# Encoder trunk, down projection: activation sums of the seven-product pairs made during the up projection and kept in device memory, and eleven such pairs per column group in place of seven

## The chip, the cores and the metric

One core of one Trainium2 chip runs the whole kernel as a single program. The metric is device microseconds from start to end of an execution: before the change 1316.85 to 1317.11 us in three runs, median 1317.1 us. The profiler saw one more execution, with a span of 1314.9 us from the first to the last instruction. PE is the engine that multiplies matrices, DVE and ACT are the two engines that work element by element, POOL is a third one that is here used mainly to issue transfers, and SP issues the loads of the weights. The program lists the instructions of each engine in a fixed order; semaphores make one engine wait for another.

## The reference

One layer of an encoder on 256 positions (T) of 2048 features (D), in float32. What matters here is the last part, the channel mixer:

```python
def conv_ffn(x, g_norm, w_up, conv_k, conv_b, w_down):
    h = rms_norm(x, g_norm)
    up = h @ w_up                                   # 2048 -> 2 * 5504
    pad = jnp.pad(up, ((0, 0), (1, 1), (0, 0)))
    up = (pad[:, :t] * conv_k[0] + pad[:, 1:t + 1] * conv_k[1]
          + pad[:, 2:t + 2] * conv_k[2] + conv_b)
    gate, val = jnp.split(up, 2, axis=-1)
    return x + (jax.nn.silu(gate) * val) @ w_down   # 5504 -> 2048
```

After it comes a last RMSNorm. Ahead of it stands the mixer block (gated MLP, neighbourhood attention, merge, output projection), which the change leaves as it is but for signs in the formulas.

## The kernel before, in words

**Products in float32.** Every operand is split into a high part (rounded to the type that PE takes) and a low part (the rest). ACT writes the high part as a copy (line 151 for weights, tile `whi`), DVE subtracts it from the original for the low part (line 152, tile `wlo`). A product is then three matmuls: high by high, low by high, high by low. In the down projection `triple` (lines 291 to 293) issues the three.

**Units.** The weights come through one list of units. A unit of the down projection is 128 rows of `w_down` by 1024 columns, 512 KB, one load on SP's queue (line 126) into a `wraw` tile. There are five `wraw` tiles and four each of `whi` and `wlo`, used in turn. When the program reaches unit i, `begin(i)` issues first the loads up to unit i+4, then the splits up to unit i+3, and then the extra tasks that were registered for i with `at(i, ...)`. PE's matmuls of unit i follow. So DVE and ACT meet their work in exactly this order, and a split of unit i+3 or i+4 can start only when PE has left the tile of four units earlier.

**The down projection** (`g_dn`, two groups of 1024 columns, 43 units each) accumulates all 43 units in four banks C, one for each half t of the positions and half c of the columns. A plain unit is four triples, 12 matmuls. Two neighbouring units (a *pair*; q is its number in the group, i = n0 + 2q its first unit) form a product of a 2 by 2 by a 2 by 2 block matrix. For the pairs in `DOWN_QUADS` it is made with seven block products in place of eight. Their four sums of activation blocks (`act_sums`, lines 298 to 303, and their split, lines 309 and 310) and four sums of weight blocks (`weight_sums`, lines 316 to 319, and their split, lines 326 and 327, into tiles "13" and "24") are made by DVE and ACT. `run_wide` issues three triples at unit i of such a pair and four at unit i+1, of which the first two use the weight sums "13" and the other two "24". Four more banks, P, accumulate over all the seven-product pairs of the group. After the last such pair `ev_sums` adds P into the residual tile `x2` (lines 909 to 919). At the end of the first group `ev_down` adds C into `x2` (`add_down`, line 1014), and the second group's first matmuls need those banks.

In the file before, the activation sums of a pair are registered for unit i-5, their split for i-4, the weight sums for i-3, and both their splits for i-2. All these tiles lie in single rooms `h0` to `h7`, so a room is written again only after its last reader. The raw weights of a pair stay in `wraw` until the weight sums have read them.

**The up projection** (`g_up`, 22 groups of two 128-column blocks of gate and value, the last one of one) has 8 units a group and, for each group, `ev_up` as tasks in the units after it: the convolution (lines 987 to 994), the gate (lines 999 and 1000), and the split into the activations `a` (lines 485 and 486) that the down projection multiplies.

Of the kernel before, what the change touches and what calls it, by code (L numbers as in the profile page):

```python
# [8 lines left out]
F32 = mybir.dt.float32  # L9
F32R = mybir.dt.float32r  # L10
# [45 lines left out]
OUT_ORDER = (tuple(range(16)), (0, 1, 6, 7, 2, 3, 10, 11, 4, 5, 8, 9, 12, 13, 14, 15))  # L56
TURN_X2 = (13, 1)
Y_GAP = 224
DOWN_QUADS = ((4, 6, 9, 11, 14, 16, 18), (3, 5, 8, 10, 13, 15, 17))


@with_exitstack
def trunk_kernel(ctx, tc, x, norm_mix, w_in, ln_g, ln_b, w_s, b_s, rpb, w_branch, w_out,
# [105 lines left out]
    def at(i, f):  # L169
        tasks.setdefault(i, []).append(f)  # L170
# [93 lines left out]

    def wide(src, row0, order, c0, acts, quads, room, done, sums=None, odd=None):
        n0 = plan_wide(src, row0, order, c0)
        boxes = {}
        for n, q in enumerate(quads):  # L270
            i = n0 + 2 * q
            own = odd if odd and n % 2 else room
            whole[i] = whole[i + 1] = None
            units[i], units[i + 1] = 1, 2
            b = boxes[q] = {}
            if sums is None:
                b["acts"] = {}
                sum_acts_at(i - 5, i - 4, b["acts"], lambda k=order[2 * q]: ff["ap"][k // 2], room, "s")
            else:
                b["acts"] = sums[order[2 * q]]  # L280
            at(i - 3, lambda i=i, b=b: weight_sums(i, b, room))
            at(i - 2, lambda b=b, own=own: weight_sums_split(b, own))
        return ("wide", n0, order, acts, quads, boxes, done)

    def sum_acts_at(i, j, box, pair, room, name):
# [3 lines left out]
    def triple(p, x, h, l, st, sp):  # L289
# [2 lines left out]
        nc.tensor.matmul(p, xl, h, start=False, stop=False)  # L292
        nc.tensor.matmul(p, xh, l, start=False, stop=sp)  # L293

    def act_sums(a, box, room):
        w = room("f", F32)
        f = w[:, 0].rearrange("p (k t) -> p k t", k=2)
        nc.vector.tensor_add(f, a[:, :, 0, :].bitcast(F32), a[:, :, 1, :].bitcast(F32))
        s1, s2, s3, s4 = (w[:, 1, n * 128:(n + 1) * 128] for n in range(4))
        nc.vector.tensor_add(s1, f[:, 0, 128:], f[:, 1, 128:])  # L300
        nc.vector.tensor_sub(s3, f[:, 0, :128], f[:, 0, 128:])
        nc.vector.tensor_sub(s2, s1, f[:, 0, :128])
        nc.vector.tensor_sub(s4, f[:, 1, :128], s2)
        box["w"] = w

    def act_sums_split(box, room, name):
        w = box.pop("w")
        o = room(name, F32R)
        nc.scalar.activation(o[:, 0], w[:, 1], AF.Copy)
        nc.vector.tensor_sub(o[:, 1], w[:, 1], o[:, 0].bitcast(F32))  # L310
        box["s"] = [(o[:, 0, n * 128:(n + 1) * 128], o[:, 1, n * 128:(n + 1) * 128]) for n in range(4)]

    def weight_sums(i, box, room):
        r0, r1 = whole.pop(i), whole.pop(i + 1)
        t13, t24 = room("t13", F32), room("t24", F32)
        nc.vector.tensor_sub(t13[:, 0], r0[:, 1], r0[:, 0])
        nc.vector.tensor_sub(t24[:, 0], r1[:, 1], t13[:, 0])
        nc.vector.tensor_sub(t13[:, 1], r1[:, 1], r0[:, 1])
        nc.vector.tensor_sub(t24[:, 1], r1[:, 0], t24[:, 0])
        box["w"] = (t13, t24)  # L320

    def weight_sums_split(box, room):
        u = []
        for name, t in zip(("13", "24"), box.pop("w")):
            h, l = room("h" + name, F32R), room("l" + name, F32R)
            nc.scalar.activation(h, t, AF.Copy)
            nc.vector.tensor_sub(l, t, h.bitcast(F32))
            u.append((h, l))
        box["t"] = {1: [x[:, 0] for x in u[0]], 3: [x[:, 1] for x in u[0]],
                    2: [x[:, 0] for x in u[1]], 4: [x[:, 1] for x in u[1]]}  # L330

    def run_wide(g, tail=0):
        kind, n0, order, acts, quads, boxes, done = g
        n1 = n0 + len(order)
        P = C = None

        def x_of(k, t):
            a = acts(k)
            return a[:, 0, t * 128:(t + 1) * 128], a[:, 1, t * 128:(t + 1) * 128]

        def plain(i, t, c):
            h, l = split_t[i]
            triple(C[t][c], x_of(order[i - n0], t), h[:, c], l[:, c], i == n0, i == n1 - 1)

        for i in range(n0, n1 - tail):
            begin(i)
            q, r = divmod(i - n0, 2)
            if C is None:
                c = [bank() for _ in range(4)]
                C = [c[:2], c[2:]]  # L350
            if q not in quads:
                for t, c in ((0, 0), (0, 1), (1, 0), (1, 1)) if i > 1 else ((0, 0), (1, 0), (0, 1), (1, 1)):
                    plain(i, t, c)
                split_t.pop(i)
                continue
            st, sp = q == quads[0], q == quads[-1]
            k, k1 = order[2 * q:2 * q + 2]
            if r == 0:
                if st:
                    P = [bank() for _ in range(4)]  # L360
                (h0, l0), (h1, l1) = split_t[i], split_t[i + 1]
                triple(P[0], x_of(k, 0), h0[:, 0], l0[:, 0], st, sp)
                triple(C[0][0], x_of(k1, 0), h1[:, 0], l1[:, 0], False, False)
                triple(C[0][1], boxes[q]["acts"]["s"][3], h1[:, 1], l1[:, 1], False, False)
                split_t.pop(i)
                split_t.pop(i + 1)
                continue
            S, W = boxes[q]["acts"]["s"], boxes[q]["t"]
            triple(P[1], S[0], *W[1], st, sp)
            triple(P[3], S[2], *W[3], st, sp)  # L370
            triple(P[2], S[1], *W[2], st, sp)
            triple(C[1][0], x_of(k1, 1), *W[4], False, False)
            if sp:
                done[0](P, i)
        if not tail:
            done[1](C, n1)
            return
        for t in range(NT):
            for c in range(2):
                for i in range(n1 - tail, n1):  # L380
                    if t == 0 and c == 0:
                        begin(i)
                    plain(i, t, c)
                done[1](C, t, c)
# [140 lines left out]
    def post_sums(P, x, spare):  # L525
        p1, p5, p6, p7 = P
        (x11, x12), (x21, x22) = x
        nc.scalar.activation(x11, p1, AF.Copy)
        nc.vector.tensor_add(spare, p6, x11)
        nc.vector.tensor_add(x12, p5, spare)  # L530
        nc.vector.tensor_add(x21, p7, spare)
        nc.vector.tensor_add(x22, p5, x21)

    def add_sums(ps, x):
        for t in range(NT):
            for c in range(2):
                nc.vector.tensor_add(x[t][c], ps[t][c], x[t][c])

    def ev_v_sums(P, i):
        def go():  # L540
# [358 lines left out]
    def ev_sums(j, room):  # L899
        def done(P, i):  # L900
# [5 lines left out]
            def first_half():  # L906
                ab, cd = room("t13", F32), room("t24", F32)
                m["v"], m["u3"], m["w"] = cd[:, 0], cd[:, 1], ab[:, 0]
                nc.scalar.activation(ab[:, 0], p1, AF.Copy)
                nc.vector.tensor_add(x11, p1, x11)  # L910
                nc.vector.tensor_add(ab[:, 1], p6, ab[:, 0])
                nc.vector.tensor_add(m["v"], p5, ab[:, 1])
                nc.vector.tensor_add(m["u3"], p7, ab[:, 1])
                nc.vector.tensor_add(m["w"], p5, m["u3"])

            def second_half():
                nc.vector.tensor_add(x12, x12, m["v"])
                nc.vector.tensor_add(x21, x21, m["u3"])
                nc.vector.tensor_add(x22, x22, m["w"])

            at(i + 1, first_half)
            at(i + 2, second_half)
# [50 lines left out]
    def ev_up(f0, nb):  # L973
        def done(ps, i):
            n = nb
            a = []
            for p in ps:
                t = tmp.tile([128, T], F32, name="tb", bufs=3)
                nc.scalar.activation(t, p[:, T:], AF.Copy)  # L979
# [18 lines left out]
            def gate(b, g, v):  # L998
                nc.scalar.activation(g, g, AF.Silu)
                nc.vector.tensor_mul(g, g, v)  # L1000
                at(cur[0] + 1, lambda: split_plain(g, ff["a"][f0 + b]))

            at(i + 1, lambda: conv(0))
            if n > 1:
# [128 lines left out]
    for f in range(0, NF, 2):  # L1133
        nb = min(2, NF - f)
        g_up.append(stationary(w_u, 0, KD, f * 128, nb * 128, 2, DFF, lambda k: rs["h", k], ev_up(f, nb)))
    h_room = {n: f"h{i}" for i, n in enumerate(("t13", "t24", "h13", "h24", "l13", "l24", "f", "s"))}

    def down_room(name, dt):
        return hpool.tile([128, 2, 512], dt, name=h_room[name])

    g_dn = [wide(w_d, 0, range(NF), g * 1024, lambda k: ff["a"][k], DOWN_QUADS[g], down_room,
                 (ev_sums(2 * g, down_room), ev_down if g == 0 else finish)) for g in range(2)]


    preload[0] = [lambda: load_x(0, 256)]
    for n, (c, _) in enumerate(X_TURN[1:]):
# [102 lines left out]
    ctx.push(fa_st)  # L1249
    ff["ap"] = [fa.tile([128, min(2, NF - k), 2, T], F32R, name=f"a{k // 2}") for k in range(0, NF, 2)]  # L1250
    ff["a"] = [ff["ap"][k // 2][:, k % 2] for k in range(NF)]
    fc = {}

    def open_conv():
# [54 lines left out]
```

## Time and profile before

| | |
|---|---|
| time, median of 3 runs | 1317.1 us (1316.85 to 1317.11) |
| profiled execution, first to last instruction | 1314.9 us |
| PE busy | 1303.3 us, 6776 matmuls |
| DVE busy | 1066.2 us |
| ACT busy | 764.8 us |
| POOL busy | 88.3 us |
| down projection on PE, start of the first and of the last matmul | 1080.30 us and 1305.36 us of the span |
| loads of `w_down` | 86 of 512 KB, median 4.6 us from issue to landing |
| granted PE clock | 0.998 of full speed over the span |

The busy time of an engine is the time in which one of its instructions ran. Matmuls overlap, so PE's busy time hides gaps shorter than a matmul's own length. A row of a timeline has the start in us from the beginning of the span, the length in us, the engine, the line of the file, the operation, the tiles out<-in, the shapes and the number of instructions; in brackets the idle time of the engine before it and whom it waited for. A row of the groups has the count, the busy time and the mean length in ns.

### The profile page before, as it was taken

How to read it: one execution, taken by the hardware profiler on the slowest of the kernel's cores; microseconds unless marked ns; L12 is line 12 of the kernel's file. 1: busy time of each engine (PE TensorE's matmuls, PEld its weight loads, DVE VectorE, ACT ScalarE, POOL GpSimd, SP SyncE). 2: the span in 40 equal slices, each digit the busy share in tenths (PEclk: the TensorE clock that was granted, in tenths of full speed). 3: DMA queues.
4: the chain of work that ended last, by engine and by line, in shares of the span. 5: the costliest groups of instructions: out<-in, count | busy, mean ns of one | idle time of the engine just before them, and what ended most of it. 6: DMA issues, size and time to landing. Idle time of an engine off the chain costs nothing.

```text
span 1314.9 us, 19329 instructions
## 1 busy us (share of the span) xinstructions
PE 1303.3 (99%) x6776; PEld 1112.0 (85%) x6776; DVE 1066.2 (81%) x1625; ACT 764.8 (58%) x1139; POOL 88.3 (7%) x176
## 2 busy tenths in 40 slices
PE   9999999999999999999999999999999999999997
PEld 7888888888888888888888888888888888888885
DVE  7996778667789966986777778787878789999997
ACT  5766476666645644556555555555656556555653
POOL 0004505323000000000000000000000000000000
PEclk9999999999999999999999999999999999999999
DMA  8768656556556657665565665656565656666663
GB/s 305 260 209 235 201 174 201 181 163 194 179 172 209 210 190 241 204 210 163 175 202 182 192 193 182 195 184 193 180 205 177 198 154 226 220 194 206 210 202 119
DMA packets 170577, 259.37 MB, mean 197 GB/s; under 512 B 12664, under 2 KB 124144, under 8 KB 170480
## 3 DMA queue, kind: packets, MB, share of 16 engines
q1 hardware_dynamic: 166448, 250.31, 59.4%
q0 software_dynamic: 3712, 7.30, 2.4%
q8 instruction: 53, 0.87, 0.3%
q10 hardware_dynamic: 320, 0.53, 0.1%
q14 instruction: 44, 0.36, 0.1%
HBM read 253.90 MB, written 2.10 MB: 195 GB/s over the span
## 4 chain that ended last, share of the span: by engine, by line
PE 97%; DVE 1%; ACT 0%; issue 0%; DMA 0%; ACTq 0%; DVEq 0%
PE bank L205 31%; PE bank L209 16%; PE bank L293 12%; PE bank L291 12%; PE bank L292 12%; PE bank L233 5%; PE bank L235 4%; PE bank L234 4%; PE bank L761 1%; DVE wlo L152 0%; PE bank L811 0%; PE bank L503 0%; PE bank L627 0%; PE bank L801 0%; PE bank L892 0%
## 5 line engine op out<-in xcount | busy, mean ns | idle before, releaser
L152 DVE TENSOR_TENSOR wlo<-wraw,whi 128x1024 fp32r<-128x1024 f32 (+1 forms) x472 | 550.3, 1178 | 188.7 <-ACT whi L151 92.0
L151 ACT ACTIVATE whi<-wraw 128x1024 fp32r<-128x1024 f32 (+1 forms) x472 | 472.0, 1015 | 204.7 <-PE bank L292 75.2
L205 PE MATMUL bank<-h,whi 128*128 128x512 f32 x1760 | 426.0, 392 | 0.0
L205 PEld LDWEIGHTS bank<-h,whi 128*128 128x128 f32 x1760 | 321.9, 188 | 62.0 <-DVE ya L631 0.3
L209 PEld LDWEIGHTS bank<-h,wlo 128*128 128x128 f32 x1760 | 225.9, 191 | 8.8
L209 PE MATMUL bank<-h,wlo 128*128 128x256 f32 x1760 | 228.6, 283 | 0.0
L989 ACT ACTIVATE tc<-ta,ck 128x256 f32<-128x256 f32 x86 | 47.1, 594 | 117.1 <-DVE ta L987 117.1
L293 PE MATMUL bank<-wlo,a 128*128 128x512 f32 x260 | 101.5, 390 | 0.2 <-DVE wlo L152 0.2
L292 PE MATMUL bank<-whi,a 128*128 128x512 f32 x260 | 101.2, 389 | 0.0
L291 PE MATMUL bank<-whi,a 128*128 128x512 f32 x260 | 101.2, 389 | 0.0
L291 PE MATMUL bank<-whi,h 128*128 128x512 f32 x204 | 80.3, 393 | 0.0
L292 PE MATMUL bank<-whi,h 128*128 128x512 f32 x204 | 79.5, 390 | 0.0
L293 PE MATMUL bank<-wlo,h 128*128 128x512 f32 x204 | 79.5, 390 | 0.0
L293 PEld LDWEIGHTS bank<-wlo,a 128*128 128x128 f32 x260 | 48.8, 188 | 11.2 <-DVE wlo L152 1.3
L292 PEld LDWEIGHTS bank<-whi,a 128*128 128x128 f32 x260 | 48.8, 188 | 10.3
L291 PEld LDWEIGHTS bank<-whi,a 128*128 128x128 f32 x260 | 48.8, 188 | 10.1
L992 DVE SCALAR_TENSOR_TENSOR tc<-ta,ck,tc 128x255 f32<-128x255 f32 x86 | 41.4, 481 | 14.5 <-ACT tc L989 14.5
L979 ACT ACTIVATE tb<-bank 128x256 f32<-128x256 f32 x86 | 28.3, 385 | 42.2 <-PE bank L205 42.2
L233 PE MATMUL bank<-whi,y 128*128 128x512 f32 x128 | 50.5, 394 | 0.0
L233 PE MATMUL bank<-whi,h 128*128 128x512 f32 x128 | 50.4, 394 | 0.0
L235 PE MATMUL bank<-wlo,h 128*128 128x512 f32 x128 | 49.9, 390 | 0.0
L235 PE MATMUL bank<-wlo,y 128*128 128x512 f32 x128 | 49.9, 390 | 0.0
(299 smaller groups left out, 1744.1 us busy)
## 6 DMA issues: line engine op xcount, KB each, us to landing
wraw<-in_w_up_dram SPq DMA_DIRECT2D x336, 256.0 KB, 3.2
wraw<-in_w_in_dram SPq DMA_DIRECT2D x111, 512.0 KB, 4.5
wraw<-in_w_down_dram SPq DMA_DIRECT2D x86, 512.0 KB, 4.6
wraw<-in_w_in_dram SPq DMA_DIRECT2D x66, 256.0 KB, 3.2
wraw<-in_w_branch_dram SPq DMA_DIRECT2D x32, 512.0 KB, 4.5
wraw<-in_w_out_dram SPq DMA_DIRECT2D x32, 512.0 KB, 3.6
xs<-in_x_dram SPq DMA_DIRECT2D x8, 256.0 KB, 7.6
vw<-y POOLq DMA_DIRECT2D x16, 128.0 KB, 6.9
```

Of the source, the lines that this page charges most:

```text
L151: nc.scalar.activation(h[:, k, :m], w[:, k, :m], AF.Copy)
L152: nc.vector.tensor_sub(l[:, k, :m], w[:, k, :m], h[:, k, :m].bitcast(F32))
L205: nc.tensor.matmul(p, h[:, k - k0, b * 128:(b + 1) * 128], acts(k), start=k == 0, stop=k == nk - 1)
L209: nc.tensor.matmul(p[:, :T], l[:, k - k0, b * 128:(b + 1) * 128], acts(k)[:, 0, :], start=False, stop=False)
L233: nc.tensor.matmul(p, xh, h[:, kk, :m], start=st, stop=False)
L234: nc.tensor.matmul(p, xl, h[:, kk, :m], start=False, stop=False)
L235: nc.tensor.matmul(p, xh, l[:, kk, :m], start=False, stop=sp)
L291: nc.tensor.matmul(p, xh, h, start=st, stop=False)
L292: nc.tensor.matmul(p, xl, h, start=False, stop=False)
L293: nc.tensor.matmul(p, xh, l, start=False, stop=sp)
L989: nc.scalar.activation(v, u, AF.Identity, scale=ck[:, 1, ch:ch + 1], bias=ck[:, 3, ch:ch + 1])
L992: nc.vector.scalar_tensor_tensor(v[:, 1:], u[:, :T - 1], ck[:, 0, ch:ch + 1], v[:, 1:], op0=OP.mult, op1=OP.add)
```

## The change

- The four activation sums of eleven pairs (3, 5, 7, 8, 10, 12, 13, 15, 16, 18, 19 of the 21, `DOWN_PAIRS`) are made once, in the up projection, from the gated activation before its split: four 128-column operations (`act_blocks`), a split into a 128 x 2 x 512 tile (`split_plain`), and a transfer of 512 KB on POOL's queue to a tensor in device memory. These are tasks two and three units after the gate of the pair's second block.
- In both groups of the down projection these pairs take seven products. Before unit i-4 of each, `stored` loads the 512 KB of sums on POOL's queue, into room `h6` or `h7` in turn. The activation sums and their split are gone from the down projection.
- Before, there were seven seven-product pairs per group; now eleven. Some of them follow directly on one another: 7 and 8, 12 and 13, 15 and 16, 18 and 19 in the first group, 7 and 8, 12 and 13, 17 and 18 (by position) in the second. For the second of two such neighbours (`late`) the weight sums are tasks of unit i-1 in place of i-3, and the splits of "13" and "24" are tasks of units i-1 and i in place of i-2.
- The second group takes the pairs of rows in another order (`down_order`), so that its seven-product positions meet the kept pairs.
- The formulas have other signs: additions of weight blocks where there were subtractions, and signs taken back when P is added. The number of operations and their shapes are the same.
[...]

The diff, cut to its core:

```diff
-DOWN_QUADS = ((4, 6, 9, 11, 14, 16, 18), (3, 5, 8, 10, 13, 15, 17))
+DOWN_PAIRS = (3, 5, 7, 8, 10, 12, 13, 15, 16, 18, 19)
+DOWN_QUADS = (DOWN_PAIRS, (1, 3, 5, 7, 8, 10, 12, 13, 15, 17, 18))
...
-            if sums is None:
+            late = q - 1 in quads
             b = boxes[q] = {}
+            if stored:
                 b["acts"] = {}
-                sum_acts_at(i - 5, i - 4, b["acts"], lambda k=order[2 * q]: ff["ap"][k // 2], room, "s")
+                at(i - 4, lambda b=b, k=order[2 * q]: stored(k // 2, b["acts"]))
...
-            at(i - 3, lambda i=i, b=b: weight_sums(i, b, room))
-            at(i - 2, lambda b=b, own=own: weight_sums_split(b, own))
+            at(i - 1 if late else i - 3, lambda i=i, b=b: weight_sums(i, b, room))
+            for h in range(2):
+                at(i - 1 + h if late else i - 2, lambda b=b, own=own, h=h: weight_sums_split(b, own, h))
...
+    def act_blocks(w, a11, a21, a12, a22):
+        s3, n1, p2, s4 = (w[:, n * 128:(n + 1) * 128] for n in range(4))
+        nc.vector.tensor_sub(s3, a11, a21)
+        nc.vector.tensor_sub(n1, a22, a21)
+        nc.vector.tensor_add(p2, n1, a11)
+        nc.vector.tensor_sub(s4, a12, p2)
...
-        nc.vector.tensor_sub(t13[:, 0], r0[:, 1], r0[:, 0])
-        nc.vector.tensor_sub(t24[:, 0], r1[:, 1], t13[:, 0])
-        nc.vector.tensor_sub(t13[:, 1], r1[:, 1], r0[:, 1])
-        nc.vector.tensor_sub(t24[:, 1], r1[:, 0], t24[:, 0])
+        nc.vector.tensor_add(t13[:, 0], r0[:, 0], r0[:, 1])
+        nc.vector.tensor_add(t24[:, 1], t13[:, 0], r1[:, 1])
+        nc.vector.tensor_add(t13[:, 1], r0[:, 1], r1[:, 1])
+        nc.vector.tensor_add(t24[:, 0], r1[:, 0], t24[:, 1])
...
+    def weight_sums_split(box, room, n):
+        t, name = box["w"][n], ("13", "24")[n]
+        h, l = room("h" + name, F32R), room("l" + name, F32R)
+        nc.scalar.activation(h, t, AF.Copy)
+        nc.vector.tensor_sub(l, t, h.bitcast(F32))
...
+                if b and f0 // 2 in ff["kept"]:
+                    at(cur[0] + 2, sums)
+                    at(cur[0] + 3, sums_split)
...
+            def sums():
+                own["w"] = ff["more"].tile([128, 512], F32, name="sw")
+                act_blocks(own["w"], *(own[k][:, t * 128:(t + 1) * 128] for k in range(2) for t in range(2)))
+
+            def sums_split():
+                o = ff["more"].tile([128, 2, 512], F32R, name="so")
+                split_plain(own["w"], o)
+                nc.gpsimd.dma_start(ff["kept"][f0 // 2], o.bitcast(F32))
...
+    def stored(pair, box):
+        n = ff["turn"] = ff.get("turn", -1) + 1
+        o = down_room(f"s{n % 2}", F32R)
+        nc.gpsimd.dma_start(o.bitcast(F32), ff["kept"][pair])
+        box["s"] = sums_of(o)
...
+    dram = keep("dram", space=bass.MemoryType.DRAM)
+    ff["kept"] = {p: dram.tile([128, 2, 512], F32, name=f"sums{p}") for p in DOWN_PAIRS}
...
-    nc = _bacc.Bacc("TRN2", target_bir_lowering=False, num_devices=1)
+    nc = _bacc.Bacc("TRN2", target_bir_lowering=False, num_devices=1, dynamic_dma_scratch_size=4096)
```

More of the change, by code (lines that the diff above doesn't have):

```diff
@@ L262, in run_group, with wide @@
             done(ps, b)
-    def wide(src, row0, order, c0, acts, quads, room, done, sums=None, odd=None):
+    def wide(src, row0, order, c0, acts, quads, room, done, sums=None, odd=None, stored=None):
         n0 = plan_wide(src, row0, order, c0)
@@ L298, in act_sums @@
         nc.vector.tensor_add(f, a[:, :, 0, :].bitcast(F32), a[:, :, 1, :].bitcast(F32))
[L299 to L303, printed above, removed]
+        act_blocks(w[:, 1], *(f[:, k, t * 128:(t + 1) * 128] for k in range(2) for t in range(2)))
         box["w"] = w
@@ L310, in act_sums_split, with sums_of @@
         nc.vector.tensor_sub(o[:, 1], w[:, 1], o[:, 0].bitcast(F32))
-        box["s"] = [(o[:, 0, n * 128:(n + 1) * 128], o[:, 1, n * 128:(n + 1) * 128]) for n in range(4)]
+        box["s"] = sums_of(o)
+    def sums_of(o):
+        return [(o[:, 0, n * 128:(n + 1) * 128], o[:, 1, n * 128:(n + 1) * 128]) for n in range(4)]
     def weight_sums(i, box, room):
@@ L315, in weight_sums @@
         t13, t24 = room("t13", F32), room("t24", F32)
[L316 to L319, printed above, removed]
+        nc.vector.tensor_add(t13[:, 0], r0[:, 0], r0[:, 1])
+        nc.vector.tensor_add(t24[:, 1], t13[:, 0], r1[:, 1])
+        nc.vector.tensor_add(t13[:, 1], r0[:, 1], r1[:, 1])
+        nc.vector.tensor_add(t24[:, 0], r1[:, 0], t24[:, 1])
         box["w"] = (t13, t24)
[L322 to L330, printed above, removed]
+    def weight_sums_split(box, room, n):
[3 more added lines that the diff above has]
+        nc.vector.tensor_sub(l, t, h.bitcast(F32))
+        box.setdefault("t", {}).update({m: (h[:, c], l[:, c]) for c, m in enumerate(((1, 3), (4, 2))[n])})
     def run_wide(g, tail=0):
@@ L368, in run_wide @@
             S, W = boxes[q]["acts"]["s"], boxes[q]["t"]
-            triple(P[1], S[0], *W[1], st, sp)
-            triple(P[3], S[2], *W[3], st, sp)
-            triple(P[2], S[1], *W[2], st, sp)
+            triple(P[1], S[1], *W[1], st, sp)
+            triple(P[3], S[0], *W[3], st, sp)
+            triple(P[2], S[2], *W[2], st, sp)
             triple(C[1][0], x_of(k1, 1), *W[4], False, False)
@@ L528, in post_sums @@
         nc.scalar.activation(x11, p1, AF.Copy)
-        nc.vector.tensor_add(spare, p6, x11)
+        nc.vector.tensor_sub(spare, x11, p6)
         nc.vector.tensor_add(x12, p5, spare)
@@ L536, in add_sums @@
             for c in range(2):
-                nc.vector.tensor_add(x[t][c], ps[t][c], x[t][c])
+                (nc.vector.tensor_sub if c else nc.vector.tensor_add)(x[t][c], ps[t][c], x[t][c])
     def ev_v_sums(P, i):
@@ L910, in first_half @@
                 nc.vector.tensor_add(x11, p1, x11)
-                nc.vector.tensor_add(ab[:, 1], p6, ab[:, 0])
+                nc.vector.tensor_sub(ab[:, 1], ab[:, 0], p6)
                 nc.vector.tensor_add(m["v"], p5, ab[:, 1])
@@ L916, in second_half @@
             def second_half():
-                nc.vector.tensor_add(x12, x12, m["v"])
+                nc.vector.tensor_sub(x12, x12, m["v"])
                 nc.vector.tensor_add(x21, x21, m["u3"])
-                nc.vector.tensor_add(x22, x22, m["w"])
+                nc.vector.tensor_sub(x22, x22, m["w"])
             at(i + 1, first_half)
@@ L976, in done @@
             a = []
+            own = {}
             for p in ps:
@@ L1001, in gate @@
                 at(cur[0] + 1, lambda: split_plain(g, ff["a"][f0 + b]))
+                own[b] = g
+                if b and f0 // 2 in ff["kept"]:
[8 more added lines that the diff above has]
+                nc.gpsimd.dma_start(ff["kept"][f0 // 2], o.bitcast(F32))
             at(i + 1, lambda: conv(0))
@@ L1135, in trunk_kernel, with down_order @@
         g_up.append(stationary(w_u, 0, KD, f * 128, nb * 128, 2, DFF, lambda k: rs["h", k], ev_up(f, nb)))
-    h_room = {n: f"h{i}" for i, n in enumerate(("t13", "t24", "h13", "h24", "l13", "l24", "f", "s"))}
+    h_room = {n: f"h{i}" for i, n in enumerate(("t13", "t24", "h13", "h24", "l13", "l24", "s0", "s1"))}
     def down_room(name, dt):
         return hpool.tile([128, 2, 512], dt, name=h_room[name])
-    g_dn = [wide(w_d, 0, range(NF), g * 1024, lambda k: ff["a"][k], DOWN_QUADS[g], down_room,
-                 (ev_sums(2 * g, down_room), ev_down if g == 0 else finish)) for g in range(2)]
+    def stored(pair, box):
+        n = ff["turn"] = ff.get("turn", -1) + 1
+        o = down_room(f"s{n % 2}", F32R)
+        nc.gpsimd.dma_start(o.bitcast(F32), ff["kept"][pair])
+        box["s"] = sums_of(o)
+    def down_order(g):
+        free = [p for p in range(NF // 2) if p not in DOWN_PAIRS]
+        kept = list(DOWN_PAIRS)
+        pairs = [(kept if q in DOWN_QUADS[g] else free).pop(0) for q in range(NF // 2)]
+        return tuple(2 * p + kk for p in pairs for kk in range(2)) + (NF - 1,)
+    g_dn = [wide(w_d, 0, down_order(g), g * 1024, lambda k: ff["a"][k], DOWN_QUADS[g], down_room,
+                 (ev_sums(2 * g, down_room), ev_down if g == 0 else finish), stored=stored) for g in range(2)]
+    dram = keep("dram", space=bass.MemoryType.DRAM)
+    ff["kept"] = {p: dram.tile([128, 2, 512], F32, name=f"sums{p}") for p in DOWN_PAIRS}
     preload[0] = [lambda: load_x(0, 256)]
@@ L1251, in trunk_kernel @@
     ff["a"] = [ff["ap"][k // 2][:, k % 2] for k in range(NF)]
+    ff["more"], more_st = pool("more")
+    ctx.push(more_st)
     fc = {}
```

## The prediction

> **What bounds the kernel now.** I read the page first: busy time by engine and the chain that ended last.
>
> ```profile
> span 1314.9 us, 19329 instructions
> PE 1303.3 (99%) x6776; PEld 1112.0 (85%) x6776; DVE 1066.2 (81%) x1625; ACT 764.8 (58%) x1139; POOL 88.3 (7%) x176
> PE 97%; DVE 1%; ACT 0%; issue 0%; DMA 0%; ACTq 0%; DVEq 0%
> ```
>
> PE is the chain. A matmul taken away is worth its full time, as long as what feeds PE keeps pace. So the second view is busy time by stretch of the span: the up projection, then the down projection, then the end.
>
> ```profile
> core 0: us, PE busy (x) PEld busy (x) DVE busy (x) ACT busy (x) POOL busy (x), PEclk, DMA share, GB/s
> 0.00:20.00 20.00, 18.32 (x90) 15.24 (x91) 11.97 (x24) 11.81 (x21) 0.70 (x6) 1.00 0.90 327
> 800.00:900.00 100.00, 100.00 (x574) 88.23 (x574) 76.60 (x126) 56.59 (x91) 0.00 (x0) 1.00 0.61 192
> 1100.00:1120.00 20.00, 20.00 (x90) 16.56 (x89) 19.83 (x29) 11.81 (x13) 0.00 (x0) 1.00 0.63 211
> 1120.00:1140.00 20.00, 20.00 (x90) 16.57 (x89) 19.14 (x27) 11.93 (x14) 0.00 (x0) 1.00 0.61 206
> 1303.00:1315.00 12.00, 2.75 (x13) 1.94 (x11) 6.61 (x19) 3.72 (x8) 0.00 (x0) 0.80 0.49 175
> ```
>
> DVE is idle for 23.4 of 100 us in the up projection, and for 0.17 of 20 us in the down projection. There it keeps up with nothing to spare, and the waits of the down projection show that it does keep up:
>
> ```profile
> PE bank L293 <- DVE wlo L152: 0.2, 1, 0.2
> ```
>
> PE waited once, for 0.2 us. Whether it will still be so decides this change. The third view is therefore the timeline of DVE over one seven-product pair and what follows (start, length), with ACT's answers, then the end of the first group.
>
> ```profile
> 1105.08 0.68 DVE L298 TENSOR_TENSOR h<-a 128x512 f32<-128x512 f32 x1
> ...
> 1106.74 1.22 DVE L152 TENSOR_TENSOR wlo<-wraw,whi 128x1024 fp32r<-128x1024 f32 x1
> 1107.88 0.68 DVE L310 TENSOR_TENSOR h<-h,h 128x512 fp32r<-128x512 f32 x1
> 1108.48 0.69 DVE L152 TENSOR_TENSOR wlo<-wraw,whi 128x512 fp32r<-128x512 f32 x1
> 1109.08 0.69 DVE L316 TENSOR_TENSOR h<-wraw 128x512 f32<-128x512 f32 x1
> 1109.80 0.69 DVE L317 TENSOR_TENSOR h<-wraw,h 128x512 f32<-128x512 f32 x1
> 1110.41 0.69 DVE L318 TENSOR_TENSOR h<-wraw 128x512 f32<-128x512 f32 x1
> 1111.01 0.69 DVE L319 TENSOR_TENSOR h<-wraw,h 128x512 f32<-128x512 f32 x1
> 1111.61 1.22 DVE L152 TENSOR_TENSOR wlo<-wraw,whi 128x1024 fp32r<-128x1024 f32 x1
> 1112.75 2.35 DVE L327 TENSOR_TENSOR h<-h,h 128x1024 fp32r<-128x1024 f32 x2
> 1115.02 3.49 DVE L152 TENSOR_TENSOR wlo<-wraw,whi 128x1024 fp32r<-128x1024 f32 x3
> ...
> 1181.71 0.68 DVE L910 TENSOR_TENSOR x<-bank,x 128x512 f32<-128x512 f32 x1
> ...
> 1184.96 1.22 DVE L152 TENSOR_TENSOR wlo<-wraw,whi 128x1024 fp32r<-128x1024 f32 x1
> 1186.09 0.69 DVE L917 TENSOR_TENSOR x<-x,h 128x512 f32<-128x512 f32 x1
> ...
> 1187.90 2.35 DVE L152 TENSOR_TENSOR wlo<-wraw,whi 128x1024 fp32r<-128x1024 f32 x2
> ```
>
> ```profile
> 1111.19 2.01 ACT L326 ACTIVATE h<-h 128x1024 fp32r<-128x1024 f32 x2 [2.15 <-DVE h L318]
> ...
> 1184.52 1.07 ACT L151 ACTIVATE whi<-wraw 128x1024 fp32r<-128x1024 f32 x1 [1.65 <-PE bank L292]
> 1187.24 1.07 ACT L151 ACTIVATE whi<-wraw 128x1024 fp32r<-128x1024 f32 x1 [1.65 <-PE bank L292]
> ```
>
> The prices, from start to start. On PE: with plain units only, ACT is let go by PE every 1187.24 - 1184.52 = 2.72 us, so a plain unit of 12 matmuls takes 2.72, a matmul 0.227, a triple 0.68. On DVE: a 1024-wide split 1.14 (1111.61 to 1112.75), a 512-wide one 0.60, the four activation sums 1.66 (1105.08 to 1106.74) and their split 0.60, the four weight sums 2.53 (1109.08 to 1111.61), both their splits 2.27, the five additions of P 3.25 (1181.71 to 1184.96), the other three 1.81. From the first weight sum to ACT's start on "13" pass 1111.19 - 1109.08 = 2.11. The last two rows also show the look-ahead used up: ACT has the weights and still waits until PE leaves the `whi` of four units earlier.
>
> **The change part by part.**
>
> *Matmuls.* Per pair one triple less; 22 such pairs in place of 14: 8 x 0.68 = 5.4 us off PE.
>
> *DVE's sum in the down projection.* A seven-product pair took 1.66 + 0.60 + 0.60 + 1.14 + 2.53 + 2.27 = 8.80; without the activation sums 6.54. A plain pair takes 2.27. Per group before 7 x 8.80 + 14 x 2.27 + 1.14 = 94.5, after 11 x 6.54 + 10 x 2.27 + 1.14 = 95.8, to which come about 10 us of additions into the residual, unchanged. PE's group shrinks from 43 x 2.72 - 7 x 0.68 = 112.2 to 109.5. So DVE has just enough time in total. It lacks it in places: a seven-product pair gives DVE 6.54 us of work and PE only 4.76.
>
> *Two such pairs in a row.* This is where I put the loss. Let 0 be the moment when PE ends the last plain unit before them (unit i-3, where i is the first unit of the second, late pair). PE then needs the low part of "13" after units i-2, i-1 and i and two matmuls: 2.04 + 2.72 + 2.04 + 0.45 = 7.25. DVE's order is fixed: low part of i+1, low part of i+2, weight sums, low "13", low part of i+3, low "24". The first can't be early, since ACT's high part of i+1 goes into the tile that PE leaves at 0.
>
> ```profile
> L151 ACT ACTIVATE whi<-wraw 128x1024 fp32r<-128x1024 f32 x71 | 72.6, 1051 | 28.8 <-PE bank L292 16.8 <-issue 5.2 <-DVE wlo L152 4.4
> L326 ACT ACTIVATE h<-h 128x1024 fp32r<-128x1024 f32 x28 | 28.2, 1054 | 21.3 <-DVE h L318 21.2
> L327 DVE TENSOR_TENSOR h<-h,h 128x1024 fp32r<-128x1024 f32 x28 | 32.9, 1218 | 0.0
> ```
>
> High i+1 ends at 1.05, with the handover 1.10; low i+1 and i+2 until 3.38; 2.11 until ACT starts on "13", at 5.49, and 1.05 until it ends; low "13" from 6.58, ended (1.22) at 7.80. PE waits 0.55. Low "24" starts at 6.58 + 1.14 + 1.14 = 8.86 and ends at 10.08; PE, going on at 7.80, needs it six matmuls later, at 9.16, and waits 0.92. That is 1.47 us for each late pair. There are four in the first group and three in the second: 7 x 1.47 = 10.3. In the trace pairs never touch, so no row shows it. Bounds: 0, if DVE were 1.5 us further ahead than the tiles allow; 2 x (6.54 - 4.76) = 3.6 each, 25 us, if none of the excess of both pairs were carried by the look-ahead. I keep 1.47, which follows the rows one by one.
>
> *The handover between the groups.* Before, the last seven-product pair of group one is 18; now 19, a late one. From the start of its low "24" DVE has without a pause: 1.14, two low parts 2.28, five additions 3.25, a low part 1.14, three additions 1.81, a half low part 0.60, the weight sums of the second group's pair 1, 2.53, and then the first addition of C, 0.69: 13.4. PE waited for the 1.22 of "24" and has 4 matmuls and 3 plain units, 9.1, until it wants C's bank: it waits 13.4 - 1.2 - 9.1 = 3.1. Bounds 0 and, should DVE come later by one low part and a half, 4.8.
>
> At the end of group two the last such pair moves from 17 to 18, one pair nearer to the last four units; I take 0, bounded by the 1.5 of one late pair.
>
> *Sums in the up projection.* Eleven times four 128-wide operations and one 512-wide split, at most 1.66 + 0.60 on DVE and under 1 us on ACT, and 0.55 us of POOL for the store. Cover: a group has 64 wide and 64 narrow matmuls, 128 of the 574 that ran in 100 us, so 22 us, in which DVE idles 23.4%, 5.2 us. Cost 0; if that cover were gone, 11 x 2.3 = 25 us at most. The store's landing is waited for by nobody before the loads, tens of us later.
>
> *Loads of the sums.* 22 of 512 KB, which SP's queue doesn't see. POOL can issue one only when PE has left the room of two kept pairs earlier, which is at the latest when PE starts unit i-4.
>
> ```profile
> L126 SPq DMA_DIRECT2D wraw<-in_w_down_dram x80: 327/328/367, 1083.5 to 1286.3; - x80
> ...
> DMA to landing us min/median/max: 3.5/4.6/6.4
> ```
>
> ```profile
> L927 POOL DMA_DIRECT2D x<-in_x_dram x4: 704/711/728, 512.7 to 514.8; - x4
> ...
> DMA to landing us min/median/max: 6.4/7.8/10.4
> ```
>
> A 512 KB transfer of POOL lands after 7.8 us, 10.4 at most. PE needs the sums two triples into unit i, 2.04 + 2.72 + 5.44 + 1.36 = 11.6 after unit i-4 began: hidden, with 1 us to spare at worst. The 45 MB of the stage become 57 MB, in some 233 us 243 GB/s, below the 327 of the span's start. But a late pair holds its raw weights until its sums, 1.5 us after PE begins it, and lets three of the five tiles go at once: three loads behind one another, beside the sums for the next pair. At 327 GB/s each is 1.6 us: the first lands at 4.6 to 6.2, the next ones 1.6 apart. The slack of the first is about 5.3. I take 1 us for the seven together; bounds 0 and 7 x 1.6 = 11.
>
> [...]
>
> [...] Four weight sums stay four, so 0. The order of rows changes addresses only. [...]
>
> **Sum.** -5.4 + 10.3 + 3.1 + 1.0 = +9.0 us. The profiled 1314.9 stands 2.2 below the median of 1317.1, which I take as constant: 1326.1.
>
> The clock is 1.00 in all stretches where PE works, and 0.80 in the last, where it mostly rests. [...]
>
> **Rivals.** *Totals decide (faster).* DVE's 105.5 us fit in PE's 109.5, and the excess of a late pair is carried by work done ahead. For it: DVE is 96 to 99% busy now and PE never waits. Against it: the rows in which ACT waits for PE's tiles. It decides if low "13" and low "24" come 1.5 us earlier than I have them; then only the matmuls count: 1317.1 - 5.4 = 1311.7. *The loads decide (much slower).* The bursts after late pairs delay every following split by a transfer: 1326.1 + 10 = 1336, more if sums land late too. For it: landings of 6.4 and 10.4 in the rows; against it: 243 of 327 GB/s. *The gain is eaten, no more.* Half the waits: -5.4 + 6.7 + 0.5 = +1.8, or 1318.9.
>
> **How the numbers follow.** Waits of late pairs as worked out, 1320 to 1333: 0.66. Loads decide, 1333 and above: 0.14. Gain eaten, within 0.2% (2.6 us, about what a measurement of this kernel can tell from no change): 0.05; a little more, to 1320: 0.02. Totals decide: 0.13. So slower 0.82, same 0.05, faster 0.13. The range from 1318.5 to 1337 leaves out the faster case and the far end of the loads. Of the likeliest case alone it is 1320 to 1333.
>
> **What would show it.** In the profile after, PE should wait for DVE's L-part of "13" and "24" twice in each of the second pairs, 0.5 and 0.9 us, seven times; for the addition of C once, by about 3 us; nowhere in the up projection. The chain of waits should hold these DVE lines in place of PE alone. Loads of `w_down` should land later than 4.6 in the median. I am wrong if PE runs through the late pairs, if POOL's loads of sums release PE, or if the up projection has grown.

## The result: slower by 0.9%, most of it where neighbours stand

The changed kernel takes 1328.15 us (median of 4 runs, 1327.76 to 1330.34) against 1316.97 before (1316.53 to 1317.11): a ratio of 1.0089, 95% interval 1.0075 to 1.0104, or 11.2 us more. Forecast were 1326.1, 9.0 us more, with a range of 1318.5 to 1337. The profiled execution spans 1326.8 us against 1314.9.

The page of the changed kernel, busy time and the chain that ended last:

```profile
PE 1303.5 (98%) x6752; PEld 1106.2 (83%) x6752; DVE 1088.3 (82%) x1644; ACT 776.1 (58%) x1152; POOL 106.8 (8%) x209
PE 90%; DVE 5%; issue 2%; ACT 2%; DMA 1%; POOL 0%; ACTq 0%; DVEq 0%; POOLq 0%
```

24 matmuls are gone, as forecast, yet PE's share of the chain fell from 97% to 90%: DVE, ACT and a transfer now stand in it. The waits of PE name them (us in total, times, longest):

```profile
PE bank L296 <- DVE h L335: 7.5, 14, 0.6
PE bank L294 <- DMA h<-sums: 2.3, 1, 2.3
...
PE bank L296 <- DVE l L335: 1.2, 2, 0.7
PE bank L206 <- DVE ya L637: 0.8, 1, 0.8
PE bank L294 <- ACT h L334: 0.4, 1, 0.4
```

Fourteen waits for the splits of weight sums, two in each of the seven late pairs; one for a load of sums, which was not forecast; and three kinds that lie ahead of the up projection, where nothing was forecast; of these only the last was there before (0.6 us). (PE's other wait of over 0.3 us, 1.4 for POOL at the start, is that of before.) Line 335 is the file's new place of the split that stood at line 327. The first late pair (units of pairs 7 and 8) in the timeline of ACT, DVE and PE:

```profile
1119.94 2.01 ACT L152 ACTIVATE whi<-wraw 128x1024 fp32r<-128x1024 f32 x2 [1.51 <-issue]
1125.45 1.06 ACT L334 ACTIVATE h<-h 128x1024 fp32r<-128x1024 f32 x1 [3.49 <-DVE h L327]
```

```profile
1121.04 2.36 DVE L153 TENSOR_TENSOR wlo<-wraw,whi 128x1024 fp32r<-128x1024 f32 x2 [0.64 <-ACT whi L152]
1123.32 0.69 DVE L325 TENSOR_TENSOR h<-wraw 128x512 f32<-128x512 f32 x1
...
1126.54 1.23 DVE L335 TENSOR_TENSOR h<-h,h 128x1024 fp32r<-128x1024 f32 x1 [0.61 <-ACT h L334]
1127.69 1.22 DVE L153 TENSOR_TENSOR wlo<-wraw,whi 128x1024 fp32r<-128x1024 f32 x1
1128.82 1.22 DVE L335 TENSOR_TENSOR h<-h,h 128x1024 fp32r<-128x1024 f32 x1
```

```profile
1127.82 0.50 PE L296 MATMUL bank<-h,h 128*128 128x512 f32 x1 [0.48 <-DVE h L335]
...
1130.10 0.50 PE L296 MATMUL bank<-h,h 128*128 128x512 f32 x1 [0.61 <-DVE h L335]
```

Set 1119.94, where ACT gets its tile, to 0: the low part of i+1 starts at 1.10, the weight sums at 3.38, ACT's "13" at 5.51, low "13" at 6.60, low "24" at 8.88. The prediction had 1.10, 3.38, 5.49, 6.58 and 8.86.

The sum of the profiled executions, from PE's starts: late pairs 11.7 us (what the distance from one matmul's start to the next has above 0.227), the load of sums 2.5, the down projection starts 2.7 later (1082.98 against 1080.30), and 24 matmuls fewer are -5.4: 11.5 of the 11.9.

The handover between the groups, where 3.1 us were forecast, cost nothing. DVE's addition of the first group's C and PE's matmul that opens the second group:

```profile
1201.64 2.48 DVE L1034 TENSOR_TENSOR x<-bank,x 128x512 f32<-128x512 f32 x4
```

```profile
1199.18 0.39 PE L296 MATMUL bank<-wlo,a 128*128 128x512 f32 x1
1199.41 0.39 PE L294 MATMUL bank<-whi,a 128*128 128x512 f32 x1
1199.64 0.39 PE L295 MATMUL bank<-whi,a 128*128 128x512 f32 x1
```

PE opens the second group at 1199.41, in step, 2.2 us before DVE begins to empty the first group's C. So the new C can't lie in the old one's banks; of the program's eight banks it must lie in the four of P, which DVE read for the last time at 1195.65. The traces don't name banks: this is concluded from the times.

### The profile page after: what moved, and what is told of

It reads as the page before. It is cut to its first block, busy times and chain, and to the rows that moved or that the text cites. A ratio compares the mean times of both kernels' runs of the same rounds, so it can differ in the third digit from the quotient of the medians.

```text
span 1326.8 us, 19441 instructions
## 1 busy us (share of the span) xinstructions
PE 1303.5 (98%) x6752; PEld 1106.2 (83%) x6752; DVE 1088.3 (82%) x1644; ACT 776.1 (58%) x1152; POOL 106.8 (8%) x209
## 4 chain that ended last, share of the span: by engine, by line
PE 90%; DVE 5%; issue 2%; ACT 2%; DMA 1%; POOL 0%; ACTq 0%; DVEq 0%; POOLq 0%
PE bank L206 30%; PE bank L210 16%; PE bank L296 9%; PE bank L294 9%; PE bank L295 9%; PE bank L234 4%; PE bank L236 4%; PE bank L235 4%; DVE wlo L153 2%; DVE h L335 1%; DMA h<-sums 1%; ACT h L334 1%; ACT whi L152 1%; PE bank L767 1%; PE bank L817 0%
## 5 line engine op out<-in xcount | busy, mean ns | idle before, releaser
L294 PE MATMUL bank<-whi,h 128*128 128x512 f32 x212 | 83.5, 394 | 2.3 <-DMA h<-sums 2.3
L296 PE MATMUL bank<-wlo,a 128*128 128x512 f32 x212 | 82.8, 390 | 0.2 <-DVE wlo L153 0.2
L296 PE MATMUL bank<-wlo,h 128*128 128x512 f32 x212 | 82.6, 390 | 0.0
L295 PE MATMUL bank<-whi,h 128*128 128x512 f32 x212 | 82.6, 389 | 0.0
L294 PE MATMUL bank<-whi,a 128*128 128x512 f32 x212 | 82.5, 389 | 0.0
L295 PE MATMUL bank<-whi,a 128*128 128x512 f32 x212 | 82.5, 389 | 0.0
L334 ACT ACTIVATE h<-h 128x1024 fp32r<-128x1024 f32 x44 | 44.9, 1053 | 60.0 <-DVE h L327 49.3
L335 DVE TENSOR_TENSOR h<-h,h 128x1024 fp32r<-128x1024 f32 x44 | 52.4, 1220 | 4.3 <-ACT h L334 4.3
L234 PE MATMUL bank<-whi,y 128*128 128x512 f32 x128 | 50.5, 394 | 0.0
L234 PE MATMUL bank<-whi,h 128*128 128x512 f32 x128 | 50.4, 394 | 0.0
L1021 POOL DMA_DIRECT2D sums<-so x11 | 6.0, 541 | 548.2 <-DVE so L492 503.4
L236 PE MATMUL bank<-wlo,h 128*128 128x512 f32 x128 | 49.9, 390 | 0.0
L235 PE MATMUL bank<-whi,y 128*128 128x512 f32 x128 | 49.8, 389 | 0.0
```

Of the source, the lines that this page charges most:

```text
L234: nc.tensor.matmul(p, xh, h[:, kk, :m], start=st, stop=False)
L235: nc.tensor.matmul(p, xl, h[:, kk, :m], start=False, stop=False)
L236: nc.tensor.matmul(p, xh, l[:, kk, :m], start=False, stop=sp)
L294: nc.tensor.matmul(p, xh, h, start=st, stop=False)
```

## The experiments

My theory: what a late pair waits for is the length of DVE's queue between the moment PE frees a tile and the splits, so the place of the weight sums in that queue decides, not the amount of work, the rooms or the transfers. Two more sources were seen in the trace: the first stage and POOL's queue. The kernel before ran beside each set; its medians there were 1316.5 to 1316.8.

**The first stage.** `wide` serves also the first stage, whose `V_QUADS` are 5 and 6: neighbours. The change makes pair 6 late there too.

```diff
-            late = q - 1 in quads
+            late = stored and q - 1 in quads
```

> The later tasks of the second of two neighbouring pairs are kept to the down projection; the first stage's pair 6, which follows pair 5, gets its weight sums and splits back at units i-3 and i-2. Theory: the 2.7 us by which the down projection starts later in the changed kernel come from that pair, 1.7 of them at 48.8 us of the span and the rest behind it, so 1328.15 - 2 = about 1326. Rival: the early 2.7 us are chance of the profiled execution, then 1328.

Measured 1326.22, 1.9 less, or 1.5 if each is taken against the kernel before beside it; the intervals of the two ratios, 1.0075 to 1.0104 and 1.0062 to 1.0092, overlap. What settles it is the trace: the rows for `l L335` and `ya L637` are gone from PE's waits, and the down projection starts at 1080.22, where it did before the change. The late rule in the first stage cost some 1.5 to 1.9 us by the medians, 2.7 in the profiled execution.

**POOL's queue.**

```diff
-            fin["load"]()
...
             at(i + 4 + j, lambda j=j: columns(j))
+            at(i + 24 + j, lambda: fin["load"]())
```

> The last two loads of the norm gain are issued on POOL's queue 20 units later, everything else as in the changed kernel. Theory: the one wait of PE for a load of sums (2.4 us at 1229 us) is POOL's queue standing still behind a gain load that waits for DVE, so it goes: 1328.15 - 2.5 = about 1325.7. Rival: that load was slow because the transfers are crowded, then 1328.

Measured 1326.45, 1.7 less (1.2 beside the kernel before); between the medians of e3 and e6 below, the same edit is worth 2.5. The wait for `h<-sums` is gone. The queue of POOL in the changed kernel (start, length, in brackets its wait):

```profile
1217.84 0.54 POOL L1307 DMA_DIRECT2D gfin<-in_norm_final_dram  x1 [26.32 <-DVE x L1042]
1220.18 0.54 POOL L1307 DMA_DIRECT2D gfin<-in_norm_final_dram  x1 [1.80 <-DVE x L1042]
1220.72 1.06 POOL L1164 DMA_DIRECT2D h<-sums  x2
```

The load of the last norm's gain waits 26 us for DVE to be done with the tile it overwrites, and two loads of sums stand behind it. The first of them was wanted at 1226.6, and PE got it at 1229.04.

Why the edit brings less than the 2.5 us of the wait shows in the next late pair of e2:

```profile
1237.12 1.06 ACT L152 ACTIVATE whi<-wraw 128x1024 fp32r<-128x1024 f32 x1 [1.20 <-DMA wraw<-in_w_down_dram]
1242.60 0.50 PE L294 MATMUL bank<-h,h 128*128 128x512 f32 x1 [0.80 <-ACT h L334]
```

ACT waits there for a load of weights, which in the changed kernel had landed by then, since PE had stood still for the sums; there ACT waits 2.09 us for PE instead. With its two further waits PE loses 2.7 us in that pair, against 1.6 in the changed kernel: 1.1 of the 2.5 us only moved.

**The place of the weight sums.** With e1's edit:

```diff
-            at(i - 1 if late else i - 3, lambda i=i, b=b: weight_sums(i, b, room))
+            at(i - 3, lambda i=i, b=b: weight_sums(i, b, room))
```

> As e1, and the weight sums of every late pair stand at unit i-3 again; only their splits stay at i-1 and i. Theory: PE's two waits in each late pair are the length of DVE's chain from the tile that PE leaves to the splits, of which the weight sums are 2.1 us, more than the 1.6 us that a late pair waits; without them in the chain the waits go, 7 x 1.6 = 11 us less than e1, about 1315. Rival: the splits wait for the single rooms of 13 and 24, which PE still reads in the pair before; then the waits stay, 1326. Second rival: DVE has too much work in all; then the wait only moves, 1322 to 1326.

Measured 1315.42 (1313.91 to 1317.77), 10.8 below e1. No wait for L335 is left in PE's waits of the down projection; only the load of sums is:

```profile
PE bank L294 <- DMA h<-sums: 2.4, 1, 2.4
```

The splits stayed where they were and write the same single rooms, so the rooms were not what PE waited for. The ten times spread over 4 us; the last section has what the trace of one of them shows, and against the faster half of them the edit is worth 11.9.

**No neighbours.** With e1's edit:

```diff
-DOWN_PAIRS = (3, 5, 7, 8, 10, 12, 13, 15, 16, 18, 19)
-DOWN_QUADS = (DOWN_PAIRS, (1, 3, 5, 7, 8, 10, 12, 13, 15, 17, 18))
+DOWN_PAIRS = (3, 5, 7, 9, 11, 13, 15, 17, 19)
+DOWN_QUADS = (DOWN_PAIRS, (1, 3, 5, 7, 9, 11, 13, 15, 17))
```

> As e1, but nine pairs in each group (3 to 19 and 1 to 17, every second one) in place of eleven, so that none follows directly on another. Theory: no late pair, no such wait; 18 pairs against 14 of the kernel before are 4 x 0.68 = 2.7 us fewer on PE, the sums' one wait of 2.4 us may stay: 1314 to 1317. Rival: DVE's total or the 18 loads of sums decide; then still some us above 1317, 1320 or more.

Measured 1314.06, a ratio of 0.9982 (0.9973 to 0.9992) to the kernel before: 2.5 us less where 2.7 were counted. PE waited once, 0.6 us, for sums behind the same gain loads.

**The sums' move alone.** The kernel before's positions, with e1's and e2's edits:

```diff
+DOWN_PAIRS = (4, 6, 9, 11, 14, 16, 18)
+DOWN_QUADS = (DOWN_PAIRS, (3, 5, 8, 10, 13, 15, 17))
```

> The pair positions of the kernel before (seven in each group, none neighbours), with the sums made in the up projection and loaded from device memory, and the gain loads later as in e2. Theory: moving the sums takes work from DVE that PE did not wait for and adds work that is hidden, so no change against the kernel before: 1316 to 1317. Rival: making and storing the sums in the up projection, or their loads, cost something by themselves: 1318 or more.

Measured 1316.12, a ratio of 0.9997 (0.9988 to 1.0006): no difference. DVE's load did fall; from 1100 to 1120 us it is busy 15.18 of 20, against 19.83 before (a row has the stretch and its length, the busy time and number of instructions of PE, of PE's loading of weights, of DVE, ACT and POOL, then the granted clock, the busy share of the transfers' engines and their GB/s):

```profile
1100.00:1120.00 20.00, 20.00 (x90) 16.56 (x89) 15.18 (x16) 9.66 (x11) 1.06 (x2) 1.00 0.80 285
800.00:900.00 100.00, 100.00 (x573) 88.23 (x572) 79.78 (x136) 57.99 (x93) 1.07 (x2) 1.00 0.64 202
```

In the up projection (800 to 900 us) DVE rose from 76.60 to 79.78 of 100 and PE stayed at 100. Making, storing and loading the sums was free; by itself it also brought nothing.

**All three edits**, e1, e2 and e3 together, eleven pairs in each group:

> Eleven pairs in each group with the three edits of e1, e2 and e3 together. Theory: the late pairs' waits, the first stage's pair and POOL's queue were all that stood against the 5.4 us of matmuls; e3's 1315.4 less 2.5 of the wait for sums: 1311.5 to 1313. Rival: without the one wait DVE or the weights' loads fall behind elsewhere: 1315.

Measured 1312.96 (1312.67 to 1313.48), a ratio of 0.9973 (0.9963 to 0.9984) to the kernel before, 3.6 us less: the fastest version. DVE in its first late pair, the same instructions in another order:

```profile
1117.90 0.68 DVE L325 TENSOR_TENSOR h<-wraw 128x512 f32<-128x512 f32 x1
...
1120.44 2.35 DVE L153 TENSOR_TENSOR wlo<-wraw,whi 128x1024 fp32r<-128x1024 f32 x2
1122.71 1.22 DVE L335 TENSOR_TENSOR h<-h,h 128x1024 fp32r<-128x1024 f32 x1
1123.84 1.22 DVE L153 TENSOR_TENSOR wlo<-wraw,whi 128x1024 fp32r<-128x1024 f32 x1
1124.98 1.22 DVE L335 TENSOR_TENSOR h<-h,h 128x1024 fp32r<-128x1024 f32 x1
```

From the low part of i+1 to low "24" pass 1124.98 - 1120.44 = 4.54 us, where they were 1128.82 - 1121.04 = 7.78. Not all of that is gain, since the low part of i+1 itself now starts behind the sums. ACT got its tile at

```profile
1117.55 2.01 ACT L152 ACTIVATE whi<-wraw 128x1024 fp32r<-128x1024 f32 x2 [1.52 <-issue]
```

and from there to low "24" pass 7.43 us, where they were 8.88: 1.45 less. DVE's two idle times of the changed kernel, 0.64 us for ACT's high part and 0.61 for ACT's "13", are filled with the sums, which wait for neither.

**A deeper look-ahead.** With e1's edit:

```diff
-SPLIT_AHEAD = 3
+SPLIT_AHEAD = 4
```

> As e1, with the splits one unit further ahead (five whi and five wlo tiles in place of four), weight sums of late pairs at i-1 as in the changed kernel. Theory that the order of DVE's queue decides: the split of one more unit then stands ahead of the weight sums as well, which takes back what the earlier release gives, so little is gained: 1323 to 1329. Rival that the look-ahead is too short: the tile comes free 2.7 us earlier, more than the 1.6 that a late pair waits, so the waits go: about 1315.

Measured 1328.24, no better than e1's 1326.22. A wait of 1.7 us in the first stage is new, but the down projection by itself, from its first matmul to its last, takes 233.7 us against e1's 234.5. There PE now waits 9 times for L335 and 5 times for ACT's half of the same splits:

```profile
PE bank L296 <- DVE h L335: 4.9, 9, 0.6
PE bank L294 <- ACT h L334: 2.5, 5, 0.9
```

One more split ahead in the program is also one more split ahead of the weight sums, as the theory has it. But the edit leaves the raw tiles at five, and ACT now waits for loads of the weights 20 times, where in e1 it did so 3 times, 3.8 us in all:

```profile
ACT whi L152 <- DMA wraw<-in_w_down_dram: 22.4, 20, 3.1
```

So the run shows that a deeper look-ahead of the splits alone does not help, and not which of the two keeps it from helping. A deeper one of the loads as well was not tried.

**Twice the traffic.** As e6, with

```diff
         nc.gpsimd.dma_start(o.bitcast(F32), ff["kept"][pair])
+        nc.gpsimd.dma_start(ff["more"].tile([128, 2, 512], F32R, name="so").bitcast(F32), ff["kept"][pair])
```

> As e6, and behind each load of sums POOL loads the same 512 KB once more into a tile that nobody reads: twice the sums' traffic. Theory: transfers have room, so at most 2 us above e6, 1312 to 1315. Rival that the crowd of transfers is near its limit: the weights' loads come late in many units, 1318 or more.

Measured 1313.78, 0.8 above e6. The transfers carried 345 GB/s in a stretch where the kernel before had 206, and the weights' loads landed after 6.7 us in the median against 5.3 in e6. ACT waited for them 13 times, 13.2 us in all, against 7 times and 4.2 in e6; of that PE noticed 0.5 us, one longer wait for L335 in the first late pair:

```profile
1120.00:1140.00 20.00, 19.59 (x86) 15.87 (x85) 19.93 (x25) 11.94 (x13) 3.17 (x6) 1.00 0.91 345
```

**A place between.** As e6, but

```diff
-            at(i - 3, lambda i=i, b=b: weight_sums(i, b, room))
+            at(i - 2 if late else i - 3, lambda i=i, b=b: weight_sums(i, b, room))
```

> As e6, but the weight sums of late pairs are tasks of unit i-2, between the place of the changed kernel (i-1) and that of e6 (i-3). Theory, by the same chain: high part of i+1 1.10, low part of i+1 until 2.24, weight sums until 4.77 with 13 on ACT from 4.35 to 5.40, low part of i+2 until 5.91, low 13 ended at 7.13 against 7.25 when PE asks: no first wait. Low 24 starts at 8.19 and ends at 9.41 against 8.61: a second wait of 0.8, with the 0.1 that each restart of PE cost, seven times, 6.3 us: 1312.96 + 6.3 = about 1319. Rival that any place ahead of i-1 frees the late pairs: 1313. Rival that the waits follow the amount of DVE's work and not its order: 1313 as well, since the work is that of e6.

Measured 1318.78 against 1319 forecast. PE waits once per late pair:

```profile
PE bank L296 <- DVE h L335: 4.3, 7, 0.6
```

The first wait is all but gone (under 0.1 us is left in two pairs) and the second is there, as the chain has it; the work on DVE is that of e6, 5.8 us faster.

## Why the prediction was right, and where it was not

*Matmuls, -5.4.* Right: in e6, where little else stands, 3.6 us of it are left over, and e4's 2.7 came out as 2.5.

*Late pairs, +10.3.* The mechanism was right to 0.02 us in each step of the chain, and e3 and e10 show that the order of DVE's queue makes it: 10.8 us went with one task's place. The size was a little short, 11.7 in the profiled execution. Two small things were missing. PE starts 0.05 us after the split has ended (1127.82 after 1126.54 + 1.23). And PE restarts slowly: in each of the fourteen waits its first matmul after the wait runs 0.50 to 0.51 in place of 0.39 us, and the next starts 0.33 to 0.35 after it in place of 0.23. The slow restart after a pair's first wait is not lost, since low "24" comes when it comes; it shortens the second wait. So the waits forecast as 0.55 and 0.92 came out as 0.64 and 0.78 in the first pair (again as distance above 0.227), and only the restart after the second, 0.11, is added. With the 0.02 of the chain that is 0.19 for each pair, 1.3 us for the seven.

*Handover, +3.1.* Wrong. DVE's chain was sized well: from the start of low "24" at 1188.91 to the end of the first addition, 1201.64 + 0.69, pass 13.4 us, the figure of the prediction. The step that failed is that PE "wants C's bank": the second group's C goes where P lay. The description of the kernel says the same and is as wrong. The 3.1 us were added on top of this late pair's 1.5; PE paid only the latter. The trace before held the warning:

```profile
1192.20 2.48 DVE L1014 TENSOR_TENSOR x<-bank,x 128x512 f32<-128x512 f32 x4
```

```profile
1192.71 0.39 PE L291 MATMUL bank<-whi,a 128*128 128x512 f32 x1
```

This is the 496th matmul of the down projection, the first of the second group. PE started it without a wait, while DVE's first addition out of the old C still ran (to 1192.89).

*Loads of the sums, hidden, and weights' loads, +1.0.* The traffic was harmless, more than I allowed for: in the changed kernel ACT waits 5 times, 4.9 us in all, for loads of the weights, PE's wait for `wlo` is 0.2 us as before, and e9 doubles the traffic at 0.8 us. The weights did land later beside the sums, after 4.6 us in the median before, 5.3 in the changed kernel and 6.7 in e9, and PE hardly waited for them: the plainest case is e2's late pair with the load that came 1.20 us late. But "POOL can issue one only when PE has left the room, which is at the latest when PE starts unit i-4" was wrong: the prediction considers who waits on SP's queue and not what else POOL's holds. A gain load that waits 26 us for DVE held up two loads of sums, 2.5 us in the trace, 1.2 to 2.5 in the medians. "If POOL's loads of sums release PE" was one of the prediction's own signs of being wrong, and here it came true, once.

*The first stage, 0.* Missed. I read `late` as a rule for the down projection; it stands in a function that four more stages call, and one has neighbours: 1.5 to 1.9 us.

*Up projection, signs, 0.* Right, by e5, which stands at 0.9997 of the kernel before.

So +9.0 against +11.2 is one main term right and a little small, two of 3.1 and 1.0 that are not there, and two of 1.2 to 2.7 each that were not seen. What is not there and what was not seen nearly cancel, and that is luck; the total is better than its parts. (The 2.2 us from span to time, taken as constant, are 1.7 in the changed kernel's profiled execution, 1328.53 against 1326.8.) Of the rivals, "totals decide" falls with e10, where the work of e6 in another order costs 5.8 us more, and "the loads decide" with PE's waits in the changed kernel and with e9.

What stays open is 1.8 us: e6 is 3.6 below the kernel before, not 5.4. In its trace PE loses 2.5 us to gaps in the down projection, against 0.9 before. Half of it is in one place, the first late pair of the second group:

```profile
1236.73 0.50 PE L296 MATMUL bank<-h,h 128*128 128x512 f32 x1 [0.62 <-DVE h L335]
```

It is the pair that waited longer in e2, too. DVE has no idle time there from 1222 to 1240; why it is further behind than in the other pairs was not tested.

## What to carry to other kernels

In an in-order queue, work that waits for nothing late belongs ahead of work that waits for a tile; put behind it, it lengthens every later answer: e1 takes 10.8 us more than e3. Here one more tile of look-ahead for the splits, with no more for the loads, did not make up for that. Before costing a moved step, list all callers of the function in which it stands and everything else on the queue onto which it goes. A balance of busy times (DVE's 105.5 us in PE's 109.5) says whether a plan can fit, and the order of one critical stretch says whether it does: here the same work cost 1326 or 1315 us. And a wait that is taken away can give others behind it: in e2 removing one of 2.5 us brought 1.2 to 1.7.

## What was not expected of the hardware

In e3's profiled execution the single wait for sums was followed by slow matmuls. The PE timeline there, and the stretches around it:

```profile
1220.75 0.80 PE L294 MATMUL bank<-whi,h 128*128 128x512 f32 x1 [2.41 <-DMA h<-sums]
...
1222.19 0.63 PE L294 MATMUL bank<-h,h 128*128 128x512 f32 x1
1222.62 0.63 PE L295 MATMUL bank<-h,h 128*128 128x512 f32 x1
1223.05 0.63 PE L296 MATMUL bank<-h,h 128*128 128x512 f32 x1
```

```profile
1215.00:1220.00 5.00, 3.34 (x15) 2.44 (x13) 5.00 (x6) 3.90 (x4) 0.00 (x0) 1.00 0.96 333
1220.00:1225.00 5.00, 4.25 (x12) 3.43 (x13) 4.68 (x8) 2.27 (x3) 0.00 (x0) 0.66 0.99 371
1225.00:1230.00 5.00, 5.00 (x24) 4.14 (x23) 4.08 (x5) 2.17 (x3) 0.53 (x1) 1.00 0.86 312
```

The granted clock is 0.66 in those 5 us, and matmuls start 0.43 apart in place of 0.23 for some 3 us: about 1.6 us on top of a wait of 2.4. In the changed kernel the clock is 1.00 from 1228 to 1232, around the end of a wait of 2.3 us, and in e1, after one of 2.5, matmuls start 0.24 apart at most from the second on. So a wait of this length came with a low clock once and without it twice. The ten times of e3 suggest that it is chance: five lie from 1313.9 to 1314.7 us, with a granted clock of 0.998 over the whole span, and five from 1316.2 to 1317.8, with 0.995 to 0.997; the profiled execution is one of the latter. In e6, without that wait, all lie within 0.8 us. So it may have struck about every second execution of e3, but only one of them is seen in a trace, and no run tests what decides it. It also means that e3's median of 1315.42 lies between two groups: the five faster have a median of 1314.31, which makes e1's loss to it 11.9 in place of 10.8, and the step from it to e6 1.3 in place of 2.5.
